# Turning a tile's float16 parts by DMA in place of TensorE, in a one-core transformer layer

## The chip, the core and the metric

The kernel runs on one core of a Trainium2 chip. The core has TensorE (PE, matrix products into PSUM), VectorE (DVE), ScalarE (ACT), GpSimd (POOL) and SyncE (SP), which here issues all DMAs. Each engine works through its own list of instructions in order and waits on semaphores for the others. The metric is the device time of one execution in microseconds. PSUM has eight banks of 2 KB per partition; a 128x512 float32 tile fills one.

## The reference

One layer of a diffusion transformer with 2048 tokens of width 1024 and 256 context tokens: a bidirectional retention of four heads (128 wide) and a grouped attention of eight heads (64 wide) side by side, then an output projection, then a feed-forward part.

```python
    ret = _ret_out(ret, rg, ret_gn_g)
...
    att = _latent_attention(q.reshape(B, L, ATT_KV_HEADS, ATT_GROUP, ATT_HD), k, v, kc, vc)

    x = x + g1 * (jnp.concatenate([ret, att], axis=-1) @ w_out)

    h2 = _modulate(_rmsnorm(x, norm2_g), sh2, sc2)
    x = x + g2 * _sqrelu_mlp(h2, w_ff1, w_ff2)
```

The change concerns the line with `w_out`: the concatenated retention and attention rows, 1024 wide, times a 1024x1024 matrix.

## The kernel before

Products of float32 accuracy are made from float16 parts: a value is split into a high part (its float16 rounding) and a low part (the rest), and high x high, high x low and low x high are summed in PSUM. The output weights lie in SBUF in this form (`wo`).

The kernel first projects all tokens and stores q, k, v and the gates in device memory. Then comes the attention stage. It is written by hand as a list of steps: `on(k, phase, fn)` puts a function into phase `phase` of step `k`, and at the end a loop goes through the steps and, in each, through the phases in the order of `PHASES`:

```python
    PHASES = ("begin", "scores", "piece", "maximum", "early", "exp", "cast", "low", "chain", "pe", "values")
    PHASES += ("late", "dma")
```

Within a phase the order is that of registration. This order is each engine's program order; no planner changes it. A step handles one block of 128 keys for one group (a tile of 128 queries and one of two key heads): two products for the scores (`st`, L214 and L215), one product that serves the row maxima of the next group (`mp`, L177 and L181), on ACT the exponential (`p`, L220) and, every second step, a cast to float16 (`phi`, L224), on DVE or POOL the low part (`plo`, L233 and L231), on DVE the maximum (`nm`, L190), and every second step sixteen products with the values (`o`, L246 to L249). `st` and `mp` have two PSUM buffers each. A group takes 18 steps, a tile of queries 36. At the end of a group ACT evacuates the sums (`so`, L253 and L254), DVE makes a reciprocal (L258), and POOL combines them into the tile's attention rows `ma` (L266, L267).

Beside this run the retention of one tile per 36 steps (`retention`) and the output of one tile per 36 steps (`output_tile`), 16 tiles from the last to the first; in them `k` is the tile's own first step, and "step 24" in the text means `k + 24`. The retention's result is `oo`, gated on POOL at step 20 (L1705). Retention and output share two PSUM banks, `bank0` and `bank1` (`psX`, one buffer each); the other six belong to `st`, `mp` and `o`.

`output_tile` has these parts for all tiles but the last (tile 0, `last`): at step 24 TensorE transposes the four 128x128 blocks of the retention rows into bank 1 (L1819); at step 26 ACT copies the bank as float16 into `rh` (L1825) and at step 27 DVE subtracts to make `rl` (L1829). At steps 28, 30 and 31 the same is done for the attention rows (`ah`, `al`, L1825 and L1827), with the scale `inv`. Sixteen steps of `PLACES` then hold three products each (L1837 to L1839): eight for the first 512 columns (four with retention parts, four with attention parts) from step 28 on, eight for the second 512 from step 46 on, both accumulated in bank 0. One step after the eighth, DVE adds the result to x (`add`, L1844) and ACT squares it (`square`, L1851, with a junk result in `oat`, which is also the tile of the retention's masked scores). The second square of a tile falls on step 59, which is step 23 of the next tile. POOL then norms x (L1864), TensorE transposes it at steps 68 and 72 (L1869), DVE modulates it (L1874), POOL shifts it and it is stored for the feed-forward stage.

SyncE issues all loads and stores in the order of the `dma` phases. In the steps spoken of here it has: the store of x (step 24, for the tile before), the loads of rk and rv (25), of x (26), of qt and kt (28), of the state f (34) and of the next group's queries (L163, L164, at 0 and 18).

Of the kernel before, what the change touches and what calls it, by code (L numbers as in the profile page):

```python
# [13 lines left out]
F16 = mybir.dt.float16  # L14
BF16 = mybir.dt.bfloat16
I32 = mybir.dt.int32
AF = mybir.ActivationFunctionType
ALU = mybir.AluOpType
# [4 lines left out]
P = 128  # L23
# [28 lines left out]
def bc(ap, shape):  # L52
    return ap.to_broadcast(shape)
# [3 lines left out]
def layer_kernel(ctx: ExitStack, tc: tile.TileContext, a: dict, out: bass.AP):  # L57
    nc = tc.nc
# [83 lines left out]
    early = kp.tile([P, NK * (VW + 1)], F32, name="early", tag="wv")  # L142
    inv = kp.tile([P, 1], F32, name="inv")
# [5 lines left out]
    class Group:  # L149
# [48 lines left out]
        def turn(self, pool=None, tag="mp"):  # L198
            self.m = (pool or psS).tile([P, 4, P], F32, name="mp", tag=tag)
            for h in range(4):  # L200
                nc.tensor.transpose(self.m[:, h], self.mt[:, h], ident)

        def rows(self):
            nc.scalar.activation(self.qr[64:, 1], self.m[64:], AF.Copy, scale=1 / ROW)
# [69 lines left out]
    with ExitStack() as st, tc.manual_schedule():  # L274
# [5 lines left out]
        op = st.enter_context(tc.tile_pool(name="op", bufs=2, reuse_waits="tile"))  # L280
# [27 lines left out]
        steps = {}  # L308
# [916 lines left out]
        for n, (col, s) in enumerate(((C_RK, 5), (C_AKV, 6), (C_AQ, 12), (C_RQ, 16), (C_RV, 18), (C_RG, 26))):  # L1225
            w = weights[0, col]
            for j in range(w.n):
                at = s + (j if col != C_RV else j > 0)
# [6 lines left out]
        for n, tile_of in enumerate(GROUPS[1]):  # L1235
            b = first[0, C_RV] + 3 + n + n // 6
            rows, x = Rows([tile_of], 1), {}
# [26 lines left out]
        at = [16, 17, 18, 19, 20, 20, 21, 21, 22, 22, 39, 40, 41, 42, 44, 46, 48, 50, 52, 54, 56, 58, 60, 62]  # L1264
# [3 lines left out]
        at = [39, 40, 41] + list(range(43, 64, 2)) + list(range(66, 84))  # L1268
        for i in range(32):
            greatest_of(i, at.pop(0))  # L1270
        at = list(range(7, 18)) + list(range(36, 42)) + [43, 46, 50, 54, 57] + list(range(66, 84))
# [214 lines left out]
        for s, (g, col, m) in enumerate(units):  # L1486
            if s < 6:
                continue
            ps = psO.tile([P, 512], F32, name="pso", tag="pso")
            w = weights[g, col]  # L1490
# [17 lines left out]
    def pool(stack, name, bufs=1, **kw):  # L1508
        return stack.enter_context(tc.tile_pool(name=name, bufs=bufs, reuse_waits="tile", **kw))

    qp = pool(attn, "qp", 2)
    op = pool(attn, "op2", 2)
# [21 lines left out]
    def bank(i, shape=(P, 4, P)):  # L1534
        return psX.tile(list(shape), F32, name=f"bank{i}", tag=f"bank{i}")
# [3 lines left out]
    def on(k, phase, fn, *args):  # L1539
        events.setdefault((k, phase), []).append((fn, args))  # L1540
# [12 lines left out]
    def settle(what):  # L1553
        while what not in settled:
            link()

    def rsqrt_chain(src, n, scale, tag, chain=chain, eps=EPS):

        v, y = (sm.tile([P, n], F32, name=f"c{x}_{tag}", tag=f"c{x}_{tag}") for x in "vy")
        chain.append(lambda: nc.gpsimd.tensor_scalar(v, src, scale, eps, op0=ALU.mult, op1=ALU.add))  # L1560
        chain.append(lambda: nc.gpsimd.tensor_tensor(y, v, half[:, :n], op=ALU.pow))
        return y
# [4 lines left out]
    ats = {}  # L1567
# [35 lines left out]

    room = ctx.enter_context(ExitStack())
    rp = pool(room, "rp", side="right")
    BUFS = {"orv": 3, "ork": 2, "okw": 2, "oo": 2, "sf": 2, "sb": 2, "ma": 2}
    wo = rp.tile([P, KT, 2, D], F16, name="wo")

    def room_tile(tag, dtype=F32, shape=(P, 512)):
        return rp.tile(list(shape), dtype, name=tag, tag=tag, bufs=BUFS.get(tag, 1))  # L1610


    RF, R0 = 2 * NK, 40
    rets = {}
# [187 lines left out]
        on(k + 3, "pe", spread)  # L1802
        on(k + 4, "early", scales)

    PLACES = (28, 29, 30, 31, 32, 33, 34, 35, 46, 48, 49, 50, 52, 54, 55, 57)
    LAST = (23, 24, 25, 26, 30, 31, 32, 33, 31, 31, 32, 32, 34, 34, 35, 35)

    def output_tile(t, k, last):
        y = {}

        def fetch_x():
            y["x"] = xp.tile([P, D], F32, name="xr", tag="xr", bufs=XR)
            nc.sync.dma_start(y["x"], a["x"][0, t * P : (t + 1) * P, :])

        def transpose(w):
            src = (rets if w == "r" else ats).pop(t)
            y["ps"] = bank(1)
            for q in range(4):
                nc.tensor.transpose(y["ps"][:, q], src[:, q * P : (q + 1) * P], ident)  # L1819

        def part(w, i):
            y[w, i] = room_tile(w + "hl"[i], F16, (P, 4, P))
            scale = inv if w == "a" else 1.0
            if i == 0:
                nc.scalar.activation(y[w, 0], y["ps"], AF.Copy, scale=scale)  # L1825
            elif w == "a":
                nc.vector.scalar_tensor_tensor(y[w, 1], y["ps"], scale, y[w, 0], op0=ALU.mult, op1=ALU.subtract)  # L1827
            else:
                nc.vector.tensor_tensor(y[w, 1], y["ps"], y[w, 0], op=ALU.subtract)  # L1829

        def product(n, k):
            if k == 0:
                y["acc", n] = bank(n if last else 0, (P, 512))
            w = "ra"[k // 4]
            hi, lo = y[w, 0][:, k % 4], y[w, 1][:, k % 4]
            wh, wl = (wo[:, k, i, n * 512 : (n + 1) * 512] for i in range(2))
            mm(y["acc", n], hi, wh, start=k == 0, stop=False)  # L1837
            mm(y["acc", n], hi, wl, start=False, stop=False)  # L1838
            mm(y["acc", n], lo, wh, start=False, stop=k == KT - 1)  # L1839

        def add(n):
            c = slice(n * 512, (n + 1) * 512)
            xc = y["x"][:, c]
            nc.vector.scalar_tensor_tensor(xc, y["acc", n], sco, xc, op0=ALU.mult, op1=ALU.add)  # L1844

        def square(n):
            if n == 0:
                y["ss"] = sm.tile([P, 2], F32, name="ss", tag="ss")
            c = slice(n * 512, (n + 1) * 512)
            junk = room_tile("oat")  # L1850
            nc.scalar.activation(junk, y["x"][:, c], AF.Square, accum_out=y["ss"][:, n : n + 1])  # L1851

        def store_x():
            nc.sync.dma_start(x1_d[t], y["x"])

        def root():
            ss = y["ss"]
            chain.append(lambda: nc.vector.tensor_tensor(ss[:, :1], ss[:, :1], ss[:, 1:], op=ALU.add))
            y["r"] = rsqrt_chain(ss[:, :1], 1, 1.0 / D, "f")
            chain.append(lambda: settled.add(("f", t)))  # L1860

        def norm():
            settle(("f", t))
            nc.gpsimd.tensor_scalar(y["x"], y["x"], y["r"], 1.0, op0=ALU.mult, op1=ALU.mult)  # L1864

        def transpose_x(q):
            y["ps", q] = bank(q if t < 2 else 1)
            for i in range(4):
                nc.tensor.transpose(y["ps", q][:, i], y["x"][:, (4 * q + i) * P : (4 * q + i + 1) * P], ident)  # L1869

        def modulate(q):
            s = slice(4 * q, 4 * q + 4)
            u = y["u", q] = xp.tile([P, 4, P], F32, name="u", tag="u")
            nc.vector.tensor_tensor(u, y["ps", q], bc(a2[:, s].unsqueeze(2), [P, 4, P]), op=ALU.mult)  # L1874

        def shift_(q):
            s = slice(4 * q, 4 * q + 4)
            u = y["u", q]
            nc.gpsimd.tensor_tensor(u, u, bc(s2[:, s].unsqueeze(2), [P, 4, P]), op=ALU.add)

        def store_h(q):
            nc.sync.dma_start(h2_d[t][:, 4 * q : 4 * q + 4], y["u", q])

        steps = (20, 21, 22, 27, 28, 30) if last else (24, 26, 27, 28, 30, 31)
        for w, at in zip("ra", (steps[:3], steps[3:])):
            on(k + at[0], "pe", transpose, w)
            on(k + at[1], "cast", part, w, 0)
            on(k + at[2], "early", part, w, 1)
        on(k + 26, "dma", fetch_x)
        places = LAST if last else PLACES  # L1890
        for j, at in enumerate(places):
            on(k + at, "pe", product, j // 8, j % 8)
        for n in range(2):
            at = k + places[8 * n + 7] + 1
            on(at, "early", add, n)
            on(at if last else at + 1, "cast", square, n)
        made = at
        on(made + 1, "dma", store_x)
        on(made if last else made + 2, "late", root)
        on(k + 68 if t == 1 else made + 2 if last else made + 4, "late", norm)  # L1900
        if t < 2:
            for f in (transpose_x, modulate, shift_, store_h):
                rest.extend([(f, 0), (f, 1)])
            return made
        on(k + 68, "pe", transpose_x, 0)
        on(k + 70, "early", modulate, 0)
        on(k + 72, "pe", transpose_x, 1)
        on(k + 73, "early", modulate, 1)
        for q in range(2):
            on(k + 74 + q, "late", shift_, q)  # L1910
            on(k + 76 + q, "dma", store_h, q)
        return made
# [42 lines left out]
    for n, t in enumerate(range(NT - 1, -1, -1)):  # L1955
        made_at = output_tile(t, R0 + RF * n, n == NT - 1)
# [448 lines left out]
    with tc.manual_schedule():  # L2405
# [8 lines left out]
        k = min(events)[0]  # L2414
# [69 lines left out]
```

## Time and profile before

| | us |
|---|---|
| median of three runs | 2664.66 |
| lowest, highest | 2662.99, 2667.97 |
| profiled execution | 2665.0 |
| its span, first to last instruction | 2663.2 |

The granted TensorE clock of the profiled execution is 0.997 of full speed. The attention stage with the output tiles lies between about 660 and 1480 us from the span's start; the feed-forward stage follows.

How to read the lines: in a list by order of time, the columns are the start (us from the span's start), the duration (us), the engine, the line of the kernel, the operation, the tile written and the tiles read, the shape and a count; in square brackets stands how long the engine was idle before it and what ended that. Matmul durations are those of a pipelined engine and overlap, so that the distance of two starts says more than a duration. In the chain of work, each line is the start, the time that this piece adds to the chain, and the piece. In a group by line, the numbers behind the bar are busy time (us), mean duration of one (ns) and idle time before. In a list of DMA issues the last two columns are the size of each and the median time from issue to landing (us). SPq is SyncE's queue.

### The profile page before, as it was taken

The numbers are of one execution on the slowest core, as the hardware profiler recorded it, in microseconds if no ns is written. First come the engines' busy times: TensorE is split into PE (matmuls) and PEld (weight loads), VectorE is DVE, ScalarE is ACT, GpSimd is POOL, SyncE is SP. The second block draws the span as 40 slices with busy tenths as digits, with TensorE's granted clock in tenths as the row PEclk, the third lists the DMA queues.
The fourth block names the chain that finished last, engine by engine and source line by source line (L and its number), as shares of the span: only waits on it lengthen the run. The fifth ranks groups of instructions, "written<-read, shape, count | busy, mean of one in ns | idle before, by whom it ended". The sixth has DMA issues, their size and how long they took to land.

```text
span 2663.2 us, 45648 instructions
## 1 busy us (share of the span) xinstructions
PE 2615.4 (98%) x16745; PEld 1466.2 (55%) x16745; DVE 2028.8 (76%) x3035; ACT 1526.2 (57%) x2576; POOL 1741.0 (65%) x1355
## 2 busy tenths in 40 slices
PE   8999999998999999999999999999999999999998
PEld 5875555545666666666666444444444444444443
DVE  5778798667888888888887597888886656656686
ACT  3856343426877788888888476666665322222243
POOL 3635566545666668787887696677663666666686
PEclk9999999999999999999999999999999999999999
DMA  6776899736112123233422664677684757475453
GB/s 230 272 247 208 305 331 322 261 113 214 48 55 70 55 79 100 90 82 89 125 76 78 247 180 143 229 233 235 206 302 141 282 182 281 170 292 170 163 187 114
DMA packets 324713, 479.78 MB, mean 180 GB/s; under 512 B 82036, under 2 KB 191876, under 8 KB 320008
## 3 DMA queue, kind: packets, MB, share of 16 engines
q1 hardware_dynamic: 324472, 476.84, 54.1%
q8 instruction: 132, 2.16, 0.3%
q14 instruction: 93, 0.76, 0.1%
q10 hardware_dynamic: 16, 0.01, 0.0%
HBM read 319.79 MB, written 156.38 MB: 179 GB/s over the span
## 4 chain that ended last, share of the span: by engine, by line
PE 71%; ACT 3%; DVE 1%; DMA 1%; issue 0%; POOL 0%; SPq 0%; DVEq 0%; POOLq 0%; ACTq 0%
PE pd L2296 7%; PE pd L2297 7%; PE pd L2295 7%; PE pu L2069 7%; PE pu L2068 7%; PE pu L2070 7%; PE o L249 4%; PE st L214 4%; PE st L215 4%; PE mp L177 3%; PE o L247 2%; PE bank L1839 2%; PE bank L1837 2%; PE bank L1838 2%; ACT p L220 1%; ACT phi L224 1%
## 5 line engine op out<-in xcount | busy, mean ns | idle before, releaser
L190 DVE TENSOR_REDUCE nm<-mp 128x1 f32<-128x512 f32 x558 | 380.7, 686 | 116.7 <-PE mp L177 110.1
L231 POOL TENSOR_TENSOR plo<-p,phi 128x1024 f16<-128x1024 f32 x160 | 349.7, 2187 | 142.9 <-ACT phi L224 128.5
L220 ACT ACTIVATE p<-st 128x512 f32<-128x512 f32 x576 | 342.1, 601 | 157.7 <-PE st L215 157.1
L2068 PE MATMUL pu<-hf,w1f 128*128 128x512 f16 x896 | 339.6, 379 | 0.0
L2069 PE MATMUL pu<-hf,w1f 128*128 128x512 f16 x896 | 339.6, 379 | 0.0
L2070 PE MATMUL pu<-hf,w1f 128*128 128x512 f16 x896 | 339.6, 379 | 0.0
L2295 PE MATMUL pd<-w,uf 128*128 128x512 f16 x896 | 339.6, 379 | 0.0
L2296 PE MATMUL pd<-w,uf 128*128 128x512 f16 x896 | 339.6, 379 | 0.0
L2297 PE MATMUL pd<-w,uf 128*128 128x512 f16 x896 | 339.6, 379 | 0.0
L2315 POOL TENSOR_TENSOR y<-y,d 128x512 f32<-128x512 f32 x128 | 210.5, 1647 | 145.2 <-ACT uf L2284 98.9
L224 ACT ACTIVATE phi<-p 128x1024 f16<-128x1024 f32 x288 | 305.2, 1060 | 0.0
L233 DVE TENSOR_TENSOR plo<-p,phi 128x512 f16<-128x512 f32 x256 | 231.0, 904 | 21.5 <-ACT phi L224 9.1
L247 PE MATMUL o<-wv,plo 128*128 128x65 f16 x2304 | 230.5, 193 | 0.0
L249 PE MATMUL o<-wv,phi 128*128 128x129 f16 x2176 | 228.9, 220 | 0.0
L214 PE MATMUL st<-qr,ks 128*128 128x512 f16 x576 | 218.3, 379 | 6.5 <-ACT p L220 4.9
L247 PEld LDWEIGHTS <-plo 128*128 128x128 f16 x2304 | 205.4, 98 | 27.7 <-issue 1.9
L215 PE MATMUL st<-qr,ks 128*128 128x512 f16 x576 | 218.5, 379 | 0.0
L2307 DVE SCALAR_TENSOR_TENSOR y<-pd,scy,y 128x512 f32<-128x512 f32 x160 | 116.9, 747 | 132.3 <-PE pd L2297 131.0
L2080 DVE TENSOR_TENSOR r<-pu,r 128x512 f32<-128x512 f32 x224 | 149.8, 684 | 84.4 <-PE pu L2070 60.9
L1195 PE MATMUL pso<-wf,h_l 128*128 128x512 f16 (+1 forms) x576 | 208.2, 361 | 0.0
L1197 PE MATMUL pso<-wf,h_l 128*128 128x512 f16 (+1 forms) x576 | 208.1, 361 | 0.0
L1196 PE MATMUL pso<-wf,h_l 128*128 128x512 f16 (+1 forms) x576 | 208.1, 361 | 0.0
(389 smaller groups left out, 6131.9 us busy)
## 6 DMA issues: line engine op xcount, KB each, us to landing
wm<-in_w_ff SPq DMA_DIRECT2D x64, 512.0 KB, 7.4
u<-r SPq DMA_DIRECT2D x128, 256.0 KB, 4.2
ur<-u SPq DMA_DIRECT2D x128, 256.0 KB, 6.1
y<-x SPq DMA_DIRECT2D x64, 512.0 KB, 6.0
wf<-w2f SPq DMA_DIRECT2D x112, 256.0 KB, 2.9
w<-wf SPq DMA_DIRECT2D x28, 1024.0 KB, 10.1
w1r<-in_w_ff SPq DMA_DIRECT2D x48, 512.0 KB, 5.1
x<-y SPq DMA_DIRECT2D x48, 512.0 KB, 2.6
```

Of the source, the lines that this page charges most:

```text
L190: nc.vector.tensor_reduce(dst, src, axis=AX.X, op=ALU.max, negate=True)
L220: nc.scalar.activation(self.p[kt // 2][:, kt % 2], self.s.pop(kt), AF.Exp, scale=HD**-0.5)
L224: nc.scalar.activation(hi, self.p[j], AF.Copy)
L231: nc.gpsimd.tensor_tensor(lo, p, hi, op=ALU.subtract)
L247: mm(o[:, : HD + 1], lo[:, i, c], v[:, : HD + 1], start=False, stop=False)
L249: mm(o, hi[:, i, c], v[:, :VW], start=False, stop=last)
L2068: mm(pu[hf, i], whi, hi, start=k == 0, stop=False)
L2069: mm(pu[hf, i], whi, lo, start=False, stop=False)
L2070: mm(pu[hf, i], wlo, hi, start=False, stop=k == 3)
L2295: mm(ps, u[:, 0, b], w[:, b, 0], start=b == 0, stop=False)
L2296: mm(ps, u[:, 0, b], w[:, b, 1], start=False, stop=False)
L2297: mm(ps, u[:, 1, b], w[:, b, 0], start=False, stop=b == 3)
```

## The change

For all tiles but the last, the rows are split into float16 parts before they are transposed, and the transposes are DMAs from SBUF to SBUF. `rows` makes the parts: ACT writes the high part from `oo` or `ma` at step 24 (retention) and 28 (attention), DVE the low part one step later. `turn` has SyncE issue two transposing DMAs, in the step of the low part, which write `rh` and `rl` or `ah` and `al`. The retention's parts use the tile `oat`, the attention's a new tile `rows`; `oo` has one buffer in place of two. The first accumulator of a tile goes to bank 1, the second stays in bank 0; the transposes of x go to bank 0. The first eight places become 29 to 32 and 34 to 37. The last tile keeps its way.

```diff
-    BUFS = {"orv": 3, "ork": 2, "okw": 2, "oo": 2, "sf": 2, "sb": 2, "ma": 2}
+    BUFS = {"orv": 3, "ork": 2, "okw": 2, "oo": 1, "sf": 2, "sb": 2, "ma": 2}
...
-    PLACES = (28, 29, 30, 31, 32, 33, 34, 35, 46, 48, 49, 50, 52, 54, 55, 57)
+    PLACES = (29, 30, 31, 32, 34, 35, 36, 37, 46, 48, 49, 50, 52, 54, 55, 57)
...
+        def rows(w, i):
+            if i == 0:
+                y[w] = (rets if w == "r" else ats).pop(t)
+                y[w, "rows"] = room_tile("oat" if w == "r" else "rows", F16, (P, 2, 512))
+            row = y[w, "rows"]
+            scale = inv if w == "a" else 1.0
+            if i == 0:
+                nc.scalar.activation(row[:, 0], y[w], AF.Copy, scale=scale)
+            elif w == "a":
+                nc.vector.scalar_tensor_tensor(row[:, 1], y[w], scale, row[:, 0], op0=ALU.mult, op1=ALU.subtract)
+            else:
+                nc.vector.tensor_tensor(row[:, 1], y[w], row[:, 0], op=ALU.subtract)
+
+        def turn(w):
+            for i in range(2):
+                y[w, i] = room_tile(w + "hl"[i], F16, (P, 4, P))
+                nc.sync.dma_start(y[w, i], y[w, "rows"][:, i], transpose=True)
...
-                y["acc", n] = bank(n if last else 0, (P, 512))
+                y["acc", n] = bank(n if last else 1 - n, (P, 512))
...
-            y["ps", q] = bank(q if t < 2 else 1)
+            y["ps", q] = bank(q if t < 2 else 0)
...
-        steps = (20, 21, 22, 27, 28, 30) if last else (24, 26, 27, 28, 30, 31)
-        for w, at in zip("ra", (steps[:3], steps[3:])):
-            on(k + at[0], "pe", transpose, w)
-            on(k + at[1], "cast", part, w, 0)
-            on(k + at[2], "early", part, w, 1)
+        for w, at in (("r", 20), ("a", 27)) if last else (("r", 24), ("a", 28)):
+            if last:
+                on(k + at, "pe", transpose, w)
+                on(k + at + 1, "cast", part, w, 0)
+                on(k + at + (2 if w == "r" else 3), "early", part, w, 1)
+            else:
+                on(k + at, "cast", rows, w, 0)
+                on(k + at + 1, "early", rows, w, 1)
+                on(k + at + 1, "dma", turn, w)
```

## The prediction

> **What bounds the kernel now.** I read the page first (busy shares), then the order of time on TensorE around the transposes that go, then the chain of work that ended last in the same stretch, then ACT, DVE, POOL and SyncE there, and last the DMA issues.
>
> ```profile
> span 2663.2 us, 45648 instructions
> PE 2615.4 (98%) x16745; PEld 1466.2 (55%) x16745; DVE 2028.8 (76%) x3035; ACT 1526.2 (57%) x2576; POOL 1741.0 (65%) x1355
> ```
>
> TensorE is the bound by share, and the change takes work from it. But a share says nothing of the place. The stretch is 700 to 1440 us, where all but the first and the last of the changed tiles are made; I follow one tile, with times from the span's start. TensorE, in order of time:
>
> ```profile
> 940.76 0.38 PE L177 MATMUL mp<-ks,qr 128*128 128x512 f16 x1
> 940.98 0.60 PE L1819 MATMUL bank<-ident,oo 128*128 128x128 f32 x4
> 941.72 0.38 PE L214 MATMUL st<-qr,ks 128*128 128x512 f16 x1
> ...
> 943.49 0.38 PE L177 MATMUL mp<-ks,qr 128*128 128x512 f16 x1
> 944.19 0.38 PE L214 MATMUL st<-qr,ks 128*128 128x512 f16 x1 [0.32 <-ACT p L220]
> ...
> 945.96 0.38 PE L177 MATMUL mp<-ks,qr 128*128 128x512 f16 x1
> 946.18 0.60 PE L1819 MATMUL bank<-ident,ma 128*128 128x128 f32 x4
> 946.62 0.38 PE L1837 MATMUL bank<-wo,rh 128*128 128x512 f16 x1
> ```
>
> The times to compare are starts, because the durations overlap. A 128x512 product takes 0.22 (940.76 to 940.98), four transposes 0.44 (946.18 to 946.62). So after the first four, at 941.42, TensorE waits 0.30 until 941.72, and after 943.71 it waits 0.48 until 944.19: 0.78 us in which it does nothing. The chain of work shows for whom:
>
> ```profile
> 939.03 0.60 ACT p L220
> 939.62 0.95 ACT phi L224
> 940.57 0.61 ACT oat L1851 x2
> 941.18 0.49 ACT p L220
> 941.67 0.28 ACT so L253
> 941.94 0.28 ACT so L254
> 942.22 0.49 ACT p L220
> 942.71 0.94 ACT phi L224
> 943.65 0.49 ACT p L220
> ...
> 944.19 0.38 PE st L214
> ```
>
> From 939.03 to 944.19 the chain lies on ACT: exponentials (p), casts (phi), the square of the tile before (oat) and the two evacuations (so). The scores at 941.72 wait for the exponential that ends at 941.67, since they have two PSUM buffers; those at 944.19 wait for the one that begins at 943.65. It is no single case; by the waits of TensorE in 700 to 1440 us:
>
> ```profile
> PE st L214 <- ACT p L220: 4.5, 14, 0.3
> ```
>
> So of each steady tile one stretch of 5.2 us is ACT's and the rest TensorE's.
>
> **The change, part by part.** *Transposes off TensorE.* Eight per tile go in 15 tiles, at 0.11 each: 0.88 per tile, 13.2 in all. The retention half (0.44) stands at 940.98, ahead of a wait that ends with ACT at 941.67: taking it away makes that wait longer and moves nothing. The attention half (0.44, at 946.18) stands where TensorE is not waiting: it counts in full. The first changed tile has no square from a tile before it and no such wait, so there I count both halves, 0.88.
>
> *The high parts on ACT.* They are still one ACT instruction per half, now from SBUF, and two steps earlier: the retention half moves from step 26 to step 24, directly behind the evacuations.
>
> ```profile
> 943.99 0.64 ACT L1825 ACTIVATE rh<-bank 128x512 f16<-128x512 f32 x1
> 944.47 0.65 ACT L220 ACTIVATE p<-st 128x512 f32<-128x512 f32 x1
> ...
> 949.95 0.60 ACT L220 ACTIVATE p<-st 128x512 f32<-128x512 f32 x1 [0.88 <-PE st L215]
> ```
> ```profile
> L72 ACT ACTIVATE hp<-hb 128x512 f16<-128x512 f32 x16 | 10.0, 626 | 0.0
> ```
>
> A copy of that size from SBUF takes 626 ns (hp<-hb), so as long as from PSUM; it holds ACT for 0.48 (943.99 to 944.47). Before, it stood behind the exponential that releases TensorE; now it stands inside the chain, ahead of two exponentials. The scores of 944.19 then start at 944.67. Afterwards ACT has the same work behind it at 944.47 as before. The attention half moves from step 30 to 28, where ACT soon idles (0.88 at 949.95): nothing. Per steady tile that is +0.48 - 0.44 = +0.04, in 14 tiles +0.6, and -0.9 for the first: -0.3 us.
>
> *The low parts on DVE, the wait of POOL.*
>
> ```profile
> 941.95 0.68 DVE L233 TENSOR_TENSOR plo<-p,phi 128x512 f16<-128x512 f32 x1
> 942.55 0.17 DVE L258 RECIPROCAL r<-so 128x4 f32<-128x4 f32 x1
> 942.64 0.66 DVE L190 TENSOR_REDUCE nm<-mp 128x1 f32<-128x512 f32 x1
> ...
> 944.66 0.69 DVE L1829 TENSOR_TENSOR rl<-bank,rh 128x512 f16<-128x512 f32 x1
> ...
> 946.09 1.48 DVE L233 TENSOR_TENSOR plo<-p,phi 128x512 f16<-128x512 f32 x1
> ```
> ```profile
> 943.22 0.61 POOL L267 TENSOR_TENSOR ma<-ma,r 128x256 f32<-128x256 f32 x1
> 943.79 2.14 POOL L231 TENSOR_TENSOR plo<-p,phi 128x1024 f16<-128x1024 f32 x1
> ```
>
> From SBUF such a subtraction takes 0.68 (941.95), or 1.48 beside other work (946.09, POOL busy). The retention one now waits from 941.95 for ACT's copy, which ends at 942.09 + 0.64 = 942.73, and runs to 943.4. Behind it wait the subtraction, the reciprocal and the reduction of 941.95 to 942.64: the reduction ends near 944.8 in place of 943.3. The third product of the step at 944.67 needs that buffer at 944.67 + 0.43 = 945.10: 0.3 to spare. POOL's L267 waits for the reciprocal and slides 1.1 us, its subtraction to 944.9 to 947.0; the values products that read it come after 947.96 (below). The attention one may take 1.48 in place of 0.74; DVE then has little room, so I take +0.05 per tile, bounds 0 and 0.74: +0.7 in 14 tiles.
>
> *DMA transposes.* Four per tile, 128 KB each, 60 in all, on SyncE's queue. SyncE runs ahead of the engines there:
>
> ```profile
> 939.96 0.78 SPq L1625 DMA_DIRECT2D orv<-rv  x1
> 940.79 0.51 SPq L1813 DMA_DIRECT2D xr<-in_x  x1
> ```
> ```profile
> h<-u SPq DMA_DIRECT2D x26, 256.0 KB, 2.0
> orv<-rv SPq DMA_DIRECT2D x14, 256.0 KB, 3.7
> oqt<-qt SPq DMA_DIRECT2D x14, 256.0 KB, 6.0
> ```
>
> The retention turn stands between these two issues. SyncE waits there for the high part (942.8), issues, waits for the low part (943.5), issues; with 0.51 to 0.78 per issue the second goes out by 943.6. Their reader is the product of step 29. It starts at 944.67 + 2.43 (the old way from 944.19 to 946.62) - 0.44 (transposes gone) + 0.65 (three more products ahead of it) = 947.31, and reads the low part at 947.74. So the second transpose has 4.1 us to land. No transposing DMA is in this trace. The nearest rows land in 2.0 us on a quiet queue and 6.0 in the thick of a burst; ahead of the turn there are only loads that have landed by 939.96 + 3.7 = 943.7, so I take 3.7, the nearest by place: no stall. At 6.0 the stall is 1.9 per tile, 28 us. It cannot be below nothing.
>
> ```profile
> L1819 PE MATMUL bank<-ident,oo x64: 272/273/278, 672.2 to 1471.5; 128*128 128x128 f32 x64
> ```
>
> From the first to the last retention transpose lie 15 x 36 - 4 = 536 steps (the last tile has it four steps earlier) and 799.3 us, 1.49 per step. The attention turn is issued at step 29 and read at step 34, 7.5 us later, and it stalls only where the first does so badly. Behind the turns wait the loads of x, q and k (4 us later) and f and the next q (some 7 us later); x is read at step 38, q and k by POOL at step 32 for products of step 42, the others later still: nothing on the path.
>
> Of the Trainium skill two passages bear on this price. "Advanced Engine Details and Errata", section X-Bar Transpose (TRN2), says that such DMAs are as fast as regular ones; by it the sum stays as it is. "VectorE: DVE Perf Modes", section The three transpose paths, gives 1309 ns for a 128x128 block by DMA against 390 ns on TensorE, and its rules say to use TensorE where PSUM will do; as an estimate, four blocks in series are 5.2 us, two DMAs in series 10.5, which would add some 5.5 us per tile. Neither can be seen in the trace of before.
>
> *Banks and places.* The first accumulator goes to bank 1, the transposes of x to bank 0, eight products move one or two steps later, and with them one addition and one square. In the code each bank's next user comes at least a step after its last reader, as before. The square moves into a stretch with the same ACT work; I take nothing, bound 0.61 (its row at 940.57) per tile.
>
> *Sum.* The profiled execution took 2665.0 us (1.8 beyond its span), 0.3 above the median of the runs. 2665.0 - 0.3 + 0.7 = 2665.4.
>
> **Rivals.** *Late landing:* the second transpose needs more than 4.1 us. For it: the row of 6.0 (oqt) in the same burst; against it: what stands ahead in the queue. At 6.0: 15 x 1.9 = 28, so 2693; at 5.0 it is 15 x 0.9 = 13, so 2678. *Blocks one after another:* if the second transpose starts only when the first has landed and each takes 6.0, the low part is there at 942.8 + 12.0 = 954.8, a stall of 7.1 per tile, 106 us: 2771. The 1309 ns per block of the Trainium skill's "VectorE: DVE Perf Modes" (The three transpose paths) would be such a mechanism. *DVE falls behind:* with the low parts at 1.48 and the wait for ACT, reductions free the PSUM buffers late; at 0.5 per tile 2673. *Faster:* ACT's copy costs the chain nothing, because ACT gets to it in an idle moment. Then the attention halves count: 14 x 0.44 + 0.88 = 7.0, so 2658; it is faster by over 0.2% from a cost of the copy below 0.06 per tile on. Against it: ACT runs in order and has no gap between 939.03 and 944.19.
>
> **How the numbers follow.** Measurement tells some 0.2% (5.3 us) from no change. As worked (gain given back, transposes in time): 0.42, range 2662 to 2669. Late landing 0.28; one after another 0.07; DVE behind 0.10: together slower 0.45. Faster 0.13. The predicted time is that of the first, 2665. The range takes in most of the faster case and late landing up to 6.0: 2657 to 2695; about 0.13 lies outside.
>
> **What would show it.** TensorE's transposes down to 8 for oo and ma. In a steady tile, the waits of the scores on ACT's exponentials grow from 0.78 to about 1.7 us; the chain then holds rh<-oo between so and p. If the products that read rh or rl wait for a DMA, landing was late; the landing column of the transposes says by how much. If the scores' wait stays near 0.78, the faster rival is right. If TensorE's mp products wait for reductions, it was DVE.

## The result and the profile after

The change makes the kernel slower by half a per cent: 2680.71 us median (2680.06 to 2680.92) against 2666.31 us, ratio 1.0053, 95% interval 1.0042 to 1.0065. The time is in the predicted range, but the likeliest case, no measurable change, did not come; the rival "DVE falls behind" did, at twice its price. That the time lies in the range at all is luck: the range reaches up to 2695 for transposes that land late, and none did.

The page of the profile after, its span and busy times:

```profile
span 2678.0 us, 45453 instructions
PE 2607.3 (97%) x16625; PEld 1454.0 (54%) x16625; DVE 2046.8 (76%) x3035; ACT 1529.4 (57%) x2576; POOL 1750.2 (65%) x1355
```

TensorE is busy 8.1 us less than before (2615.4), with 120 transposes fewer, and the span is 14.8 longer. The difference is waiting. The waits of TensorE in 700 to 1460 us (in us: total, times, longest):

```profile
PE st L214 <- ACT p L220: 16.4, 28, 0.6
PE mp L181 <- DVE nm L190: 11.4, 14, 1.7
```

The first is the wait of the scores that the prediction started from (4.5 in all, longest 0.3, in its row of before; 4.7 up to 1460). The second is all but new (before, once, 0.2): once per tile the product that serves the row maxima waits for a reduction on DVE. The chain of work of one steady tile holds both, first on ACT, then on DVE (start, time added to the chain, piece):

```profile
946.32 0.61 ACT oat L1869 x2
...
947.31 0.38 ACT so L253
947.69 0.28 ACT so L254
947.96 0.52 ACT oat L1822
...
953.27 0.67 DVE nm L190
953.94 0.93 DVE rows L1824
954.87 1.45 DVE plo L233
956.32 0.61 DVE nm L190
...
956.97 0.38 PE mp L181 x2
```

The piece at 947.96 is the retention's high part (L1822), inside ACT's chain behind the square and the two evacuations, as predicted. The pieces at 953.94 and 954.87 are the attention's low part (L1824) and a low part of the exponentials (L233). TensorE, in order of time:

```profile
955.95 0.38 PE L215 MATMUL st<-qr,ks 128*128 128x512 f16 x1
956.97 0.38 PE L181 MATMUL mp<-ks,qr 128*128 128x256 f16 x2 [0.65 <-DVE nm L190]
```

From 955.95 to 956.97 are 1.02 us, where two such products are 0.21 to 0.22 apart: a wait of 0.81. By starts (which give about 0.16 more per wait than the waits view) this wait is 0.81 us in nine tiles, 1.13 in four, and 1.80 and 1.90 in the first and the last: 15.5 in all. The scores wait 0.74 + 0.22 + 0.79 = 1.75 us per steady tile, against 0.78 before. The balance is 14 x 0.97 = 13.6 more for the scores, 15 x 0.88 = 13.2 less for the transposes, and 15.5 for the new wait: 15.9; the spans show 14.8 and the medians 14.4.

Why is DVE late? DVE and POOL at that place, in order of time:

```profile
951.90 1.43 DVE L233 TENSOR_TENSOR plo<-p,phi 128x512 f16<-128x512 f32 x1
953.26 0.68 DVE L190 TENSOR_REDUCE nm<-mp 128x1 f32<-128x512 f32 x1
953.86 1.01 DVE L1824 SCALAR_TENSOR_TENSOR rows<-ma,inv,rows 128x512 f16<-128x512 f32 x1
954.79 1.52 DVE L233 TENSOR_TENSOR plo<-p,phi 128x512 f16<-128x512 f32 x1
```
```profile
950.66 2.13 POOL L231 TENSOR_TENSOR plo<-p,phi 128x1024 f16<-128x1024 f32 x1
952.77 1.56 POOL L1882 TENSOR_SCALAR xr<-xr,cy_f 128x1024 f32<-128x1024 f32 x1
954.30 1.46 POOL L1633 TENSOR_TENSOR okw<-ork,kd 128x512 f32<-128x512 f32 x1
955.73 2.57 POOL L231 TENSOR_TENSOR plo<-p,phi 128x1024 f16<-128x1024 f32 x1
```

Add start and duration. POOL's operations end at 952.79, 954.33 and 955.76; the three subtractions on DVE end at 953.33, 954.87 and 956.31: each 0.54 or 0.55 after the POOL operation in whose time it began. These subtractions read two tiles of SBUF. The reduction, which reads PSUM, takes 0.68 beside the same POOL operations. In the kernel before, the low parts read the transposed bank in PSUM and took 0.69 (`rl`, beside POOL's L231 of 943.79, in the prediction's rows) and 0.74 (`al`). Their move to SBUF has put them into the queue for POOL.

The transposing DMAs did their part. SyncE's issues, and the DMA view (median us from issue to landing):

```profile
948.51 1.23 SPq L1831 DMA_TRANSPOSE rh<-oat  x1
949.85 1.19 SPq L1831 DMA_TRANSPOSE rl<-oat  x1
951.09 0.57 SPq L1813 DMA_DIRECT2D xr<-in_x  x1
```
```profile
oqt<-qt SPq DMA_DIRECT2D x14, 256.0 KB, 3.8
rh<-oat SPq DMA_TRANSPOSE x14, 2.5
rl<-oat SPq DMA_TRANSPOSE x14, 2.6
```

The low part lands at 949.85 + 2.6 = 952.45, and the first product that reads it starts at 953.52: 1.1 us to spare.

### The profile page after: what moved, and what is told of

The parts are those of the page before. It is cut to its first block, busy times and chain, and to the rows that moved or that the text cites. A ratio compares the mean times of both kernels' runs of the same rounds, so it can differ in the third digit from the quotient of the medians.

```text
span 2678.0 us, 45453 instructions
## 1 busy us (share of the span) xinstructions
PE 2607.3 (97%) x16625; PEld 1454.0 (54%) x16625; DVE 2046.8 (76%) x3035; ACT 1529.4 (57%) x2576; POOL 1750.2 (65%) x1355
## 4 chain that ended last, share of the span: by engine, by line
PE 82%; DVE 6%; ACT 3%; DMA 2%; issue 1%; SPq 0%; POOL 0%; DVEq 0%; POOLq 0%; ACTq 0%
PE pd L2318 7%; PE pd L2319 7%; PE pd L2317 7%; PE pu L2090 7%; PE pu L2091 7%; PE pu L2092 7%; PE pso L1195 4%; PE pso L1197 4%; PE pso L1196 4%; PE o L249 4%; PE st L214 4%; PE st L215 4%; PE mp L177 3%; PE o L247 2%; PE bank L1857 2%; PE bank L1855 2%
## 5 line engine op out<-in xcount | busy, mean ns | idle before, releaser
L231 POOL TENSOR_TENSOR plo<-p,phi 128x1024 f16<-128x1024 f32 x160 | 353.7, 2213 | 128.2 <-ACT phi L224 122.5
L233 DVE TENSOR_TENSOR plo<-p,phi 128x512 f16<-128x512 f32 x256 | 247.9, 970 | 18.9 <-ACT phi L224 8.7
```

The lines of the kernel that those rows point to most:

```text
L231: nc.gpsimd.tensor_tensor(lo, p, hi, op=ALU.subtract)
```

## The experiments

The theory from here: two independent costs, ACT's copy inside the chain and DVE's subtractions that take turns with POOL. The rivals: late landings, the banks and places, or one chain that only shows at two places. Times are medians; each ratio is to the kernel before on the same chip, which took 2665.1 to 2666.6 us.

**ACT's chain alone.** The kernel before, with an additional ACT copy of the retention rows at step 24 (and one buffer for `oo`, as in the change):

```diff
...
+        def copy():
+            nc.scalar.activation(room_tile("extra", F16), rets[t], AF.Copy)
...
+        if not last:
+            on(k + 24, "cast", copy)
```

> The kernel before, with one more ACT copy of the retention rows at step 24 of each tile but the last, into a tile that nobody reads, and one buffer for oo. If ACT holds the chain there, the scores wait 0.48 us longer in 14 tiles: +7 us, 2673 (2671 to 2675). If ACT has room there, 2666.

Measured: 2672.89 us, ratio 1.0026 (1.0016 to 1.0036). The longest wait of the scores goes from 0.3 to 0.6. An operation of 0.48 us at this place costs about 14 times 0.48 (6.7 us; the medians differ by 6.3), as the prediction's step on ACT said.

The opposite: the kernel before with the second square four steps later, out of the chain, and root and norm three steps later.

```diff
-            on(at if last else at + 1, "cast", square, n)
+            on(at if last else at + (1 if n == 0 else 5), "cast", square, n)
...
-        on(made if last else made + 2, "late", root)
-        on(k + 68 if t == 1 else made + 2 if last else made + 4, "late", norm)
+        on(made if last else made + 5, "late", root)
+        on(k + 68 if t == 1 else made + 2 if last else made + 7, "late", norm)
```

> The kernel before, with the second square of a tile (ACT, 0.61 us) moved from step 23 to step 27 of the next tile, out of ACT's chain between steps 23 and 26, and the norm of x three steps later. If that chain is what TensorE waits for (0.78 us per tile), the waits at the scores go and the time falls by up to 14 x 0.78 = 11 us, to 2656 (2654 to 2662). If the chain is a shadow of something else, 2666.

Measured: 2656.73 us, ratio 0.9969 (0.9958 to 0.998), the fastest of all kernels here. What is left of the wait, in the same stretch:

```profile
PE st L214 <- ACT p L220: 0.2, 1, 0.2
```

So most of the 0.78 us per tile that TensorE stood still before the change (8.4 of 14 x 0.78 = 10.9 us by the medians) could be had without any DMA, by taking 0.61 us of ACT's work out of the 5.2 us in which ACT sets the pace.

**DVE's subtraction alone.** The changed kernel without the attention's low part on DVE; its DMA turns the high part a second time:

```diff
-            elif w == "a":
-                nc.vector.scalar_tensor_tensor(row[:, 1], y[w], scale, row[:, 0], op0=ALU.mult, op1=ALU.subtract)
-            else:
+            elif w == "r":
                 nc.vector.tensor_tensor(row[:, 1], y[w], row[:, 0], op=ALU.subtract)
...
-                nc.sync.dma_start(y[w, i], y[w, "rows"][:, i], transpose=True)
+                nc.sync.dma_start(y[w, i], y[w, "rows"][:, i if w == "r" else 0], transpose=True)
```

> The changed kernel without DVE's attention low part: the instruction is left out, and the second attention DMA turns the high part once more, so the low products are computed with wrong numbers at the same cost. If that DVE instruction, with the queueing behind POOL that it brings, makes the mp products of step 31 wait 0.8 to 1.1 us, the wait goes and the time is 2667 (2665 to 2670), with ACT's chain as in the changed kernel. If DMAs or the banks cost it: 2680.

Measured: 2667.47 us, ratio 1.0008 (0.9999 to 1.0017). The waits of TensorE:

```profile
PE st L214 <- ACT p L220: 16.7, 29, 0.6
PE o L247 <- POOL plo L231: 1.8, 4, 0.4
PE bank L1855 <- DMA rl<-oat: 0.7, 1, 0.7
```

The wait at mp is gone, that of the scores is whole. One subtraction of 1.01 us per tile carries the 13 us by which the changed kernel is slower than this one, and the rest of the change comes out even, as the prediction's sum had it.

**The landing.** Two more transposing DMAs ahead of the retention's, into the tile `rows`, which is free there:

```diff
         def turn(w):
+            if w == "r":
+                spare = room_tile("rows", F16, (P, 2, 512)).rearrange("p i (j t) -> p i j t", j=4)
+                for i in range(2):
+                    nc.sync.dma_start(spare[:, i], y[w, "rows"][:, 0], transpose=True)
```

> The changed kernel with two more transposing DMAs per tile (into a tile nobody reads) ahead of the retention's two: SyncE holds 1.2 us for each, so the retention's parts land 2.5 us later, at 954.9 in place of 952.4 on the clock of the tile in the changed kernel's trace, where the products read them at 953.1 to 953.5. If landing has some 1.1 us to spare in the changed kernel, the products now wait 1.3 to 1.5 us per tile, DVE catches up meanwhile and the mp wait of 0.8 us goes: net +0.5 to +0.7 per tile, 2688 to 2692. If transposing DMAs cost by their traffic, more; if landing had no room in the changed kernel, 15 x 2.5 = 38 us: 2718.

Measured: 2691.98 us, ratio 1.0099 (1.0086 to 1.0113).

```profile
PE bank L1861 <- DMA rl<-oat: 10.1, 13, 1.7
PE bank L1859 <- DMA rh<-oat: 7.0, 13, 1.3
```

The first two hold SyncE for 2.53 us:

```profile
949.09 2.53 SPq L1832 DMA_TRANSPOSE rows<-oat  x2
```

Now the products wait for the DMAs, 1.40 us per steady tile by starts; the wait at mp has gone meanwhile, since TensorE comes later to it. Such waits would be seen if landing were late in the changed kernel; there are none.

**Banks and places.** The kernel before with nothing but these:

```diff
-    PLACES = (28, 29, 30, 31, 32, 33, 34, 35, 46, 48, 49, 50, 52, 54, 55, 57)
+    PLACES = (29, 30, 31, 32, 34, 35, 36, 37, 46, 48, 49, 50, 52, 54, 55, 57)
...
-            y["ps"] = bank(1)
+            y["ps"] = bank(1 if last or w == "r" else 0)
...
-                y["acc", n] = bank(n if last else 0, (P, 512))
+                y["acc", n] = bank(n if last else 1 - n, (P, 512))
...
-            y["ps", q] = bank(q if t < 2 else 1)
+            y["ps", q] = bank(q if t < 2 else 0)
```

> The kernel before with nothing of the change but its banks and places: the attention transposes and those of x in bank 0, the first accumulator in bank 1 and the second in bank 0, the first eight products at 29 to 32 and 34 to 37. If banks and places cost nothing (the prediction's step), 2664 to 2668, and the scores' waits stay at 0.30 and 0.48. Rival: a part of the change's cost is theirs; at 0.2 us per tile 2669, at the bound of 0.61 per tile 2674.

Measured: 2666.76 us, ratio 1.0002 (0.9993 to 1.0012). They cost nothing.

**Each half alone.** The changed kernel, in which one half goes the old way by TensorE:

```diff
...
-            if last:
+            if last or w == "a":
+                late = 0 if last else 1
                 on(k + at, "pe", transpose, w)
-                on(k + at + 1, "cast", part, w, 0)
-                on(k + at + (2 if w == "r" else 3), "early", part, w, 1)
+                on(k + at + 1 + late, "cast", part, w, 0)
+                on(k + at + (3 if late or w == "a" else 2), "early", part, w, 1)
```

(For the other half with `"r"` in the first line. Attention transposes by TensorE use bank 0, and the attention's low part stands at step 31 then, not 29.)

> The changed kernel with the retention half alone split as rows and turned by DMA; the attention half is transposed by TensorE at step 28 into bank 0, with its parts at 30 and 31 read from PSUM. ACT's chain keeps the copy at step 24 (+0.48 per tile), DVE's attention subtraction has one SBUF input and doesn't take turns with POOL: the wait at mp is gone, the sum is 2665 + 14 x 0.48 = 2672 (2670 to 2675). Rival: the retention subtraction, which now also has two SBUF inputs, makes the wait of DVE: 2680 and a wait at mp of 0.5 or more per tile.

Measured: 2672.01 us, ratio 1.0024 (1.0014 to 1.0033).

```profile
PE st L214 <- ACT p L220: 16.4, 28, 0.6
```

This is the only wait of TensorE that the view lists for this kernel. The retention half costs what ACT's copy costs, and its subtraction, though it also reads two SBUF tiles, keeps nobody waiting.

> The changed kernel with the attention half alone split as rows and turned by DMA; the retention half is transposed by TensorE at step 24 into bank 1, its parts at 26 and 27 read from PSUM. ACT's chain is as before the change (scores wait 0.78), eight minus four transposes cost nothing at the wait, the attention transposes' 0.44 per tile are saved (6.2), and the attention subtraction takes turns with POOL: a wait at mp of 0.8 to 1.1 per tile as in the changed kernel gives 2665 - 6 + 15 = 2674 (2670 to 2677). Rival: POOL and DVE run about 1 us earlier without the wait of the retention subtraction for ACT's copy, the wait at mp shrinks below 0.4: 2659 to 2664, faster than before.

Measured: 2683.63 us, ratio 1.0065 (1.0048 to 1.0081), 6.6 us above the upper bound expected. Two things had been left out. The scores wait a third time in a steady tile, 0.42 us by starts (at 952.64 for ACT's exponential), about what the attention transposes took that stood there: that half's 0.44 gave nothing in this kernel. And the wait at mp is there, but in nine of 14 tiles it is 1.9 us by starts, not 0.8 to 1.1; it is 0.35 in four and 1.70 in one. One with 1.9, DVE and then POOL:

```profile
954.98 2.61 DVE L233 TENSOR_TENSOR plo<-p,phi 128x512 f16<-128x512 f32 x1
```
```profile
954.71 2.34 POOL L231 TENSOR_TENSOR plo<-p,phi 128x1024 f16<-128x1024 f32 x1 [0.20 <-ACT phi L224]
```

POOL's long subtraction (L231) began 0.27 before DVE's, which then takes 2.61 and ends 0.54 after it. In the changed kernel DVE's subtraction stands at 954.79 too, but POOL began L1633 at 954.30 and L231 only at 955.73, so that DVE waited for the shorter one. Hence the halves do not add up (0.24% and 0.65% alone, 0.53% together): beside what the scores wait, the price is the length of whatever POOL has just begun, and small shifts decide which that is.

**Moving the work.** The attention's low part and its DMA at step 31 in place of 29:

```diff
...
+                low = at + (1 if w == "r" else 3)
                 on(k + at, "cast", rows, w, 0)
-                on(k + at + 1, "early", rows, w, 1)
-                on(k + at + 1, "dma", turn, w)
+                on(k + low, "early", rows, w, 1)
+                on(k + at + 1, "dma", turn, w, (0,))
+                on(k + low, "dma", turn, w, (1,))
```

> Only the attention low part (DVE) and its transposing DMA move from step 29 to step 31; everything else is the changed kernel. If the loss is DVE's work of steps 28 to 31, which makes the mp products of step 31 wait 0.8 to 1.1 us per tile, that wait goes and the time falls by about 15 x 0.85 = 13 us, to 2668 (2665 to 2671). If the DMA transposes themselves cost it (traffic, SyncE held 1.2 us per issue, loads that go out later), nothing falls: 2679 to 2682. If ACT's chain were the whole loss: also 2679 to 2682.

Measured: 2675.89 us, ratio 1.0032 (1.0021 to 1.0043): better than the change by 5 us, not by the 13 of its best case.

```profile
PE mp L201 <- DVE mt L196: 3.2, 9, 0.4
PE o L247 <- POOL plo L231: 3.0, 4, 0.8
```

The wait at L181 is gone and smaller ones stand further on. The subtraction now meets the long POOL operation:

```profile
950.82 2.41 DVE L1824 SCALAR_TENSOR_TENSOR rows<-ma,inv,rows 128x512 f16<-128x512 f32 x1
```
```profile
950.55 2.13 POOL L231 TENSOR_TENSOR plo<-p,phi 128x1024 f16<-128x1024 f32 x1
```

This also answers whether DVE merely has too much to do there. In the kernel with the retention half alone by DMA, the attention's low part stands at the same step 31 and beside the same POOL operation (L231, 952.49 to 954.62 in the tile shown; L73 in four tiles of both kernels), but reads the transposed bank in PSUM, and takes 0.74 in each of the 15 tiles, where here it takes 1.40 to 2.42:

```profile
953.07 0.74 DVE L1845 SCALAR_TENSOR_TENSOR al<-bank,inv,ah 128x512 f16<-128x512 f32 x1
```

So it is the operand's place, not DVE's load, that makes the subtraction long.

Then the same subtraction on POOL, with the scale folded into the reciprocal:

```diff
             nc.vector.reciprocal(self.r, self.so[:, :, HD])
+            nc.vector.tensor_scalar_mul(self.r, self.r, inv)
...
-                nc.vector.scalar_tensor_tensor(row[:, 1], y[w], scale, row[:, 0], op0=ALU.mult, op1=ALU.subtract)
+                nc.gpsimd.tensor_tensor(row[:, 1], y[w], row[:, 0], op=ALU.subtract)
...
```

> The changed kernel with the attention low part on POOL instead of DVE (the scale inv goes into the reciprocal, one small DVE instruction per group). POOL and the DVE instructions that read two SBUF tiles take turns in the trace; on POOL the part needs some 1.2 us in POOL's own order. If DVE's queueing is the loss and POOL has 1.2 us there, 2667 to 2670. If POOL then blocks DVE's own subtractions for 1.2 us longer, the mp wait stays: 2676 to 2684.

Measured: 2678.21 us, ratio 1.0045 (1.003 to 1.006). Now POOL is late, four times by up to 1.9 us:

```profile
PE o L247 <- POOL plo L231: 7.4, 4, 1.9
```

Next, the retention's parts two steps later, behind the exponentials that the scores wait for, with the products behind them; and then both halves two steps later:

```diff
-    PLACES = (29, 30, 31, 32, 34, 35, 36, 37, 46, 48, 49, 50, 52, 54, 55, 57)
+    PLACES = (31, 32, 33, 34, 35, 36, 37, 38, 46, 48, 49, 50, 52, 54, 55, 57)
...
-        for w, at in (("r", 20), ("a", 27)) if last else (("r", 24), ("a", 28)):
+        for w, at in (("r", 20), ("a", 27)) if last else (("r", 26), ("a", 28)):
```

> The retention parts move back to steps 26 and 27 (where the kernel before made them), their DMAs to step 27, the first eight places to 31 to 38; the attention parts stay at 28 and 29. If the copy at step 24 costs ACT's chain 0.48 us per tile, the scores' waits fall from 1.75 to about 1.25 us and the time by 14 x 0.48 = 7 us to 2674, unless DVE, which has the same work in steps 27 to 31, gives all of it back (then 2680, with the mp wait at 1.3 to 1.6). If the copy costs the chain nothing, the scores' waits stay at 1.75.

> Both kinds of parts at the steps of the kernel before: retention at 26 and 27, attention at 30 and 31, DMAs at 27 and 31, places from 31 on. If DVE's place and ACT's place are the two losses, the gain that is left is the attention transposes, 0.44 in 14 tiles, and 0.88 in the first: 7 us under the kernel before, 2659 (2657 to 2663). If DMA transposes cost something by themselves, it stays above the kernel before.

Both expectations failed. Measured: 2753.58 us, ratio 1.0322 (1.0307 to 1.0338), and with both later (`("r", 26), ("a", 30)`) 2715.47 us, ratio 1.0182 (1.0166 to 1.0197). The waits of the first:

```profile
PE mp L181 <- DVE nm L190: 31.5, 12, 2.9
PE st L214 <- ACT p L220: 15.6, 40, 0.7
PE mp L177 <- DVE nm L190: 12.9, 17, 0.9
```

Two things had been overlooked. The retention's subtraction, harmless at step 25, now also falls beside POOL's L231 and takes 1.78 us; with the 1.01, 0.92 and 2.61 of the next three, mp waits 3.03 to 3.05 by starts in nine tiles. And the first addition to x (L1862) moved with the eighth place from step 38 to 39. DVE, which works in order, stands idle before it until the eighth product is done, 0.85 us, and so comes to the next low part of the exponentials (L233) only after POOL has begun its own (DVE, then POOL):

```profile
1000.16 1.93 DVE L233 TENSOR_TENSOR plo<-p,phi 128x512 f16<-128x512 f32 x1
```
```profile
999.41 2.13 POOL L231 TENSOR_TENSOR plo<-p,phi 128x1024 f16<-128x1024 f32 x1 [2.66 <-ACT phi L224]
```

It ends at 1002.09, 0.55 after POOL's; the reduction behind it is late, and mp (L177) waits 1.03 for it, in every steady tile of both kernels. The kernel with both later also waits at L181, 0.80 in 13 tiles. Waits at L201 and L1639 and longer ones of the scores come on top; the 49 us that it lost were not followed further.

**Both costs at once.** The changed kernel with the second square later, as above, its junk result in the tile `rows`:

```diff
-            junk = room_tile("oat")
+            junk = room_tile("rows" if n and not last else "oat")
...
-            on(at if last else at + 1, "cast", square, n)
+            on(at if last else at + (1 if n == 0 else 5), "cast", square, n)
```

> The changed kernel with the second square four steps later (its unused output in the tile of the attention rows, free there), root and norm three steps later. The theory has two independent costs in the changed kernel: ACT's chain (scores wait 1.75 us per steady tile) and DVE's subtractions of two SBUF tiles that take turns with POOL (mp products wait 0.8 to 1.1). The square's 0.61 leaves the chain, the DVE wait stays: 14 x 0.6 = 8 less, 2672 (2669 to 2675), still slower than before by 0.2% or more. Rival: the waits are one chain, and what the scores no longer wait for is waited for at mp: 2679 to 2682.

Measured: 2671.8 us, ratio 1.0023 (1.0013 to 1.0032). That is the time expected, for another reason:

```profile
PE st L214 <- ACT p L220: 14.3, 29, 0.6
PE mp L181 <- DVE nm L190: 4.9, 5, 1.8
```

The scores still wait nearly as long (16.4 in the changed kernel): with the copy in its way ACT paces TensorE for longer, and the square falls into that stretch again. What went is the wait at mp, from 11.4 to 4.9. The norm on POOL (L1882) came later and stands behind L1633 now, not ahead of it:

```profile
949.83 0.68 DVE L233 TENSOR_TENSOR plo<-p,phi 128x512 f16<-128x512 f32 x1
```
```profile
949.36 2.07 POOL L1882 TENSOR_SCALAR xr<-xr,cy_f 128x1024 f32<-128x1024 f32 x1
```

DVE's L1824 has waited there for POOL's L1633, which ends at 949.37. Then DVE is served ahead of POOL: L233 takes 0.68, and POOL's L1882 2.07 where it took 1.56 in the changed kernel. So a time that agrees does not confirm the theory behind it; the two costs are separate in their causes, but an edit on ACT moved POOL and so changed the other.

## Why the prediction was right and wrong

- *What bounds the kernel, and ACT's chain: right.* The copy inside the chain costs what its 0.48 us say (2672.89 for the copy alone), and the scores' wait of "about 1.7" is 1.75. The retention's transposes gave nothing and the attention's 0.44 counted (the changed kernel's scores wait as long as those of the retention half alone, and its span is 8.3 us longer, 2678.0 against 2669.7, with 15.5 us of new wait): 0.97 more wait against 0.88 fewer transposes is +0.09 per tile, predicted +0.04.
- *The low parts on DVE: wrong, and this is the step that failed.* The prediction took "+0.05 per tile, bounds 0 and 0.74". Measured are 0.81 in nine tiles, 1.13 in four and 1.80 and 1.90 in two: 15.5 us in place of 0.7, above the upper bound. The mechanism stood among the rivals ("DVE falls behind") at 0.5 per tile with a chance of 0.10. The row that it needed was quoted, "1.48 beside other work (946.09, POOL busy)", but was read as a duration that a subtraction may have. Set beside POOL's rows it is a turn: L1864 ends at 945.91 + 1.12 = 947.03, the subtraction at 947.57, 0.54 later. The bound of 0.74 also counted one subtraction alone, whereas it pushed the next one (L233) into POOL's next operation, 1.52 us.
- *The retention's low part: right.* It takes 0.73, and by the kernel with that half alone nobody waits for it.
- *DMA transposes: right in the verdict.* The landing was assumed at 3.7 us and is 2.5 and 2.6 for the retention's two; the issue was taken at 0.51 to 0.78 and holds SyncE for 1.2. Both errors fit into the time that was there, 3.7 us from the issue to the reader by the trace (4.1 predicted). "Late landing", the largest rival with 0.28, did not occur, nor did the blocks one after another.
- *Banks and places: right,* nothing (2666.76).
- *The sum:* 2665.4 plus 15.5 - 0.7 for DVE and 14 x 0.05 for ACT is 2680.9; measured 2680.71. That it agrees to 0.2 us is luck: these terms make the change 15.9 us, and 14.4 lie between the medians.

## What to carry to other kernels

When an operand moves from PSUM to SBUF, look at what POOL does at that time: a DVE operation with two SBUF operands may have to wait for a whole POOL operation, as here, so its price is the length of that operation, and the next operations in DVE's order pay too. Compare the ends of slow operations with the ends on the other engine before bounding their cost by their longest duration. And where a bound engine waits in a stretch that another engine paces, take work of that engine out of the stretch first (here one square moved, -0.31%), for work taken from the waiting engine only makes it wait longer.

## What the hardware showed unexpectedly

Between 700 and 1440 us of the changed kernel, DVE's operations with two SBUF tiles of 128x512 take 0.68 to 0.69 where no POOL operation of over 0.3 us runs at their start. Of the 153 that begin inside one, 140 end 0.53 to 0.57 after its end, and 13 take 0.68 to 0.71 (beside operations of one column, L1561, or in the last 0.1 us of another); no other case occurs. The Trainium skill states this in "SBUF — State Buffer", section Who interferes with whom: a DVE instruction with two SBUF inputs contends with a GpSimd instruction that reads SBUF, the port pair that the two share is an exclusive lock, and the order of issue decides who blocks whom. The traces agree, in both directions: DVE's 2.61 behind POOL (the attention half alone), and POOL's 2.07 behind DVE (the square later).

A transposing DMA of 128 KB lands 2.5 to 2.6 us after its issue (the attention's high part, issued right behind three loads, 4.2), a load of 256 KB (`oqt`) in the same stretch 3.8 us. No run has a plain DMA of this size from SBUF to SBUF to set beside it. Of the two passages of the Trainium skill that the prediction weighed, this is nearer to that of "Advanced Engine Details and Errata", X-Bar Transpose (TRN2), as fast as regular DMAs, than to the prediction's estimate of 5.2 us, four blocks in series at the 1309 ns of "VectorE: DVE Perf Modes", The three transpose paths. But each holds SyncE's queue for 1.2 us, where a load or store there holds it 0.3 to 0.8, and with two more of them in front that is what delayed the products.

After the wait of 2.89 us in the kernel with the retention's parts later, TensorE ran slower for a while:

```profile
982.72 0.43 PE L181 MATMUL mp<-ks,qr 128*128 128x256 f16 x2 [2.89 <-DVE nm L190]
982.94 0.63 PE L1855 MATMUL bank<-wo,rh 128*128 128x512 f16 x1
983.37 0.63 PE L1856 MATMUL bank<-wo,rh 128*128 128x512 f16 x1
```

The starts are 0.42 to 0.43 apart in place of 0.22, until 986.36: the granted clock is 0.50 from 983 to 986, and 1.00 before and after. This follows nine of this kernel's 14 waits at L181, each time for some 3.4 us, but the length of the wait alone does not decide it. By starts, it follows seven of the ten waits of 3.0 us or more, two of the three of 2.1, and not the one of 1.8. In the kernel with two more transposing DMAs it follows twice upon a wait of 1.4 with one of 0.9 right behind it; four waits of 2.0 in the kernel with the low part on POOL do not show it. So a long wait can cost more than its own length: by an estimate from these stretches, up to 9 x 1.7 = 15 us of the 87 that this kernel lost.
